# The adaLN products of a mixer kernel in four column groups of the TensorE array

## The chip, the cores and the metric

The kernel runs on one core of a Trainium2 chip. The metric is device time in microseconds (us) of one execution; the kernel before took 1698.51 us, the median of three runs (1695.80 to 1698.83).

## The reference

One layer of an encoder works on 1280 tokens of 1024 channels (a prompt of 1024 rows and a sample of 256, each with its own condition vector c). What the change touches is the first step: a vector of shift and scale for each of the two conditions, which modulates the normalised input ahead of the large projection.

```python
def mixer_layer(x, c, w_ada, b_ada, norm_g, w_in, ...):
    mod = c @ w_ada + b_ada                       # c: (1, 1024), w_ada: (1024, 3072)
    shift, scale, gate = jnp.split(mod[:, None, :], 3, axis=-1)
    h = rms_norm(x, norm_g) * (1.0 + scale) + shift
    p = h @ w_in                                  # (tokens, 1024) @ (1024, 11280)
...
    merged = g_conv * (y_conv @ w_proj_conv) + g_mlstm * (y_m @ w_proj_mlstm)
    return x + gate * (merged @ w_out)
```

All of it is float32. A gated short convolution and a bidirectional mLSTM follow from p; they and the output stage are untouched.

## The kernel before

**The large projection.** h is kept transposed: 1024 channels as eight tiles `xt` of 128 channels, by 1280 tokens in two halves of 640 (columns of the program `b11`, `b12` for the channels 0 to 511, `b21`, `b22` for 512 to 1023). The projection runs as a Strassen scheme on pairs of 128 output columns: seven jobs a pair, each a product of four channel tiles (k = 0 to 3) with 640 tokens. Every operand is split into a rounded part H and a remainder L, so one k of one job is six matmuls of 128x320 (line 770), written `L770 ... wh/wl` below. I call these six **a group**. The moving operands of the jobs are `b00H/L` (that is b11), `b10H/L` (b21), `t2H/L`, `t3H/L`, further `xt` tiles (t1 and t4) and `b11H/L` (b22). The first eight jobs, the "corners", use only b11 and then b21, with weights that were loaded ahead (`raw`, two loads of 256 KB each).

**The beginning.** `beginning()` loads w_ada's shift and scale columns in eight parts, here w0 to w7 (`load_wa(i)`, two loads of 512 KB each: two k tiles, 512 shift and 512 scale columns). w0 to w3 give the first 512 channels, w4 to w7 the second 512. Between them it loads the ten tiles of x. They land in tiles that later hold other things, so the trace shows w5 as `b10H`, w6 as `b10L`, w4 and w7 both as `b11H`; x appears as `t3H`, `t3L`, `b11L`, `t2H`, `t2L`.

**adaLN.** `adaln(i)` multiplies c with part i: for each of two k tiles and each half j (shift, scale) one fp32 matmul with a 128x4 stationary operand `cz4` (two condition columns, two of zeros) and 512 moving columns, accumulated over w0..w3 or w4..w7 into a PSUM tile `acc` of 4 rows in two banks (line 487). After the last part the two 4x512 rows go to SBUF, one by VectorE, one by ScalarE (line 496), are turned into columns by four TensorE transposes each (line 500) and `modulation` makes `s1` and `shf` from them (lines 474 to 476).

**The turns.** `turn_x` transposes one channel tile of two or three token tiles (line 449, 128x128 each) into a PSUM tile `misc`, of which there are two, and ScalarE or VectorE writes it to `xt` with scale and shift (lines 454, 457). `both_parts` splits an `xt` tile into H (ScalarE, 381) and L (VectorE, 382), `combine` forms sums of tiles (VectorE, 387). VectorE also makes sums of weights (`comb`, 642) and adds finished jobs (686).

**What sets the order.** All operations are put on a `Board` with an estimated duration; `order()` plays them by ready times and steps and fixes the order of every engine's queue, and of SyncE's queue (SP), which issues all the loads and stores. The estimates decide the order only; on the chip each engine takes its queue strictly as written and waits for semaphores. The names with numbers in the order rows are buffers.

Of the kernel before, what the change touches and what calls it, by code (L numbers as in the profile page):

```python
# [9 lines left out]
F32 = mybir.dt.float32  # L10
F32R = mybir.dt.float32r
AF = mybir.ActivationFunctionType
ALU = mybir.AluOpType
# [3 lines left out]
P = 128  # L17
D = 1024
KT = D // P
# [21 lines left out]
class Board:  # L41
# [25 lines left out]
    def buf(self, pool, shape, dt, tag, bufs, t=None):  # L67
        b = self.Buf(pool, shape, dt, tag, bufs, t)
        self.places.setdefault((id(pool), tag), []).append(b)
        return b  # L70

    def op(self, eng, us, f, r=(), w=(), after=(), low=False, slack=0.0):

        o = self.Op()
        o.eng, o.us, o.f, o.low, o.step, o.n, o.played, o.slack = eng, us, f, low, self.step, len(self.ops), False, slack
        o.before = set(after)
        for t in r:
            if t in self.writer:
                o.before.add(self.writer[t])
        for t in w:  # L80
            o.before.update(self.readers.get(t, ()))
            if t in self.writer:
                o.before.add(self.writer[t])
        for t in w:
            self.writer[t], self.readers[t] = o, []
        for t in r:
            if t not in w:
                self.readers.setdefault(t, []).append(o)
        o.before.discard(o)
        o.bufs = list(dict.fromkeys(b for t in (*r, *w) for b in (t if isinstance(t, tuple) else (t,)) if isinstance(b, self.Buf)))  # L90
        for b in o.bufs:
            b.users.append(o)
        self.ops.append(o)
        return o
# [87 lines left out]
def encoder_kernel(  # L182
# [7 lines left out]
    V, A, G, PE = nc.vector, nc.scalar, nc.gpsimd, nc.tensor  # L190
# [14 lines left out]
    const = ctx.enter_context(tc.tile_pool(name="const", bufs=1))  # L205
# [20 lines left out]
    ident = const.tile([P, P], F32, name="ident")  # L226
# [67 lines left out]
    s1 = const.tile([P, KT, 2], F32, name="s1")  # L294
    shf = const.tile([P, KT, 2], F32, name="shf")
    board = Board()
    op, buf = board.op, board.buf
# [5 lines left out]
    cp = xstack.enter_context(tc.tile_pool(name="cp", bufs=5))  # L303
# [86 lines left out]
    def beginning():  # L390
        junks = [((lambda b=b: b[:, 0:D]), b) for b in (big(), big())]

        def cz4():
            return junks[0][1][:, D:D + 32].rearrange("p (k s) -> p k s", s=4)

        def load_wa(i):

# [65 lines left out]
        cv_ = cols[:, 0:16].rearrange("p (s k) -> p k s", s=2)  # L463
        ctok = ("c",)
        op("POOL", .15, lambda: G.memset(cz4(), 0.0), w=[junks[0][1], ctok])
        op("DVE", .15, lambda: V.tensor_copy(cz4()[:, :, 0:2], cv_), r=[ctok], w=[ctok])
        pada = {}

        def modulation(hf, pm):

            ks = slice(4 * hf, 4 * hf + 4)
            pmc = pm[:, 0:32].rearrange("p (h k l s) -> p h k l s", h=2, l=2, s=2)[:, :, :, 0]
            wide = (lambda c: cols[:, c + 4 * hf:c + 4 * hf + 4].unsqueeze(2).to_broadcast([P, 4, 2]))
            V.tensor_tensor(out=s1[:, ks], in0=pmc[:, 1], in1=wide(RSH + 8), op=ALU.add)
            V.scalar_tensor_tensor(out=s1[:, ks], in0=s1[:, ks], scalar=1.0, in1=wide(RNG), op0=ALU.add, op1=ALU.mult)
            V.tensor_tensor(out=shf[:, ks], in0=pmc[:, 0], in1=wide(RSH), op=ALU.add)

        def adaln(i):

            hf = i // 4  # L480
            if i == 0:
                pada.update((n, buf(psX, [P, 2, 512], F32, "acc", 3)) for n in range(2))
            t = pada[hf]
            for n, (wa, tok) in enumerate(wa_at[i]):
                kt = 2 * (i % 4) + n
                for j in range(2):
                    op("PE", .88, lambda j=j, kt=kt, wa=wa: PE.matmul(
                        t[0:4, j, :], cz4()[:, kt, :], wa()[:, j * 512:(j + 1) * 512],
                        start=kt == 0, stop=kt == KT - 1), r=[ctok, tok], w=[(t, j)])
            if i % 4 < 3:  # L490
                return
            pm = misc_buf()
            for j in range(2):
                m, f = buf(cp, [P, 4, P], F32, "comb", 5), (V.tensor_copy, A.copy)[j]
                row = (lambda m=m: m[0:4].rearrange("p a b -> p (a b)"))
                op(("DVE", "ACT")[j], .6, lambda j=j, f=f, row=row: f(row(), t[0:4, j, :]), r=[(t, j)], w=[m])

                def turn_mod(j=j, row=row):
                    for r in range(4):
                        PE.transpose(pm[:, 16 * j + 4 * r:16 * j + 4 * r + 4], row()[:, r * P:(r + 1) * P], ident[0:4, 0:4])  # L500

                op("PE", .25, turn_mod, r=[m], w=[(pm, j)])
            op("DVE", .6, lambda: modulation(hf, pm), r=[(pm, 0), (pm, 1)], w=[("s1", hf)])

        def fetch(*items):

            for it in items:
                board.step = -20
                if it[0] == "x":
                    for c in GROUPS[it[1]]:  # L510
                        load_x(c)
                    board.step = -14 if it[1] < 2 else -11
                    norm_x(GROUPS[it[1]])
                elif it[0] == "w":
                    load_wa(it[1])
                    board.step = -18 + it[1] // 4 * 16
                    adaln(it[1])
                else:
                    early_load(*it)
# [55 lines left out]
    def big():  # L575

        return buf(rp, [P, T], F32, "big", 2)

    def misc_buf():
        return buf(psA, [P, 512], F32, "misc", 2)  # L580
# [651 lines left out]
    for st in head_pairs(range(1, NH)):  # L1232
        add(st)

    beginning()
    advance(ends[0] - 10)
    board.step = at[0]
# [26 lines left out]
    for k in range(at[0], len(todo)):  # L1264
        n, m = divmod(k - at[0], 7)
# [365 lines left out]
    def second(s):  # L1631
        h, i = divmod(s - 10, 10)
        return (h, two_[h].order[i], i) if 0 <= h < NH else (None, None, None)
# [3 lines left out]
    for s in range(10 * NH + 15):  # L1637
# [4 lines left out]
        h, c, i = second(s - 3)  # L1642
        if h is not None and h + 2 < NH and c in (5, 7, 9):
            load_head(h + 2, (5, 7, 9).index(c))
        h, i = divmod(s, 10)
# [11 lines left out]
        h, c, i = second(s)  # L1657
        if h is not None:
            g = c - c % 2
# [7 lines left out]
        h, c, i = second(s - 2)  # L1667
        if h is not None:
            prs[h, c - c % 2].values(c)
        h, c, i = second(s - 4)  # L1670
# [185 lines left out]
```

## Time and profile before

| | |
|---|---|
| runs | 1698.51 us median, 1695.80 lowest, 1698.83 highest |
| span of the profiled execution, first to last instruction | 1694.4 us |
| own time of the profiled execution | not given apart; the runs lie 1.4 to 4.4 us above the span |
| TensorE (PE) busy | 1654.8 us, 98% of the span |
| VectorE (DVE), ScalarE (ACT), GpSimd (POOL) busy | 59%, 34%, 40% |
| products of line 770 on the chain that ended last | 61% of the span |
| DMA in the first of 40 slices, and mean | 318 GB/s, 143 GB/s |
| mean granted TensorE clock | 0.996 of full speed |

The profile's page gives for each engine its busy time, for 40 slices of the span its busy tenths, and the chain of work that ended last, followed back step by step to what released it. Its other views, asked for stretches of the trace, list instructions in order of time with their duration and, in brackets, the idle time of the engine before them and what ended it (`[0.88 <-DVE xt L382]`: 0.88 us idle until VectorE's line 382 had written `xt`). An `x8` at the end means that eight such records are merged in the row. A full fp32 matmul leaves two records, a transposition or an fp32r matmul one. Busy times of PE overlap, since its ends are modelled: its starts are the sounder numbers.

### The profile page before, as it was taken

What the parts mean: (1) busy time and instruction counts of PE and PEld (TensorE: products, weight loads), DVE (VectorE), ACT (ScalarE), POOL (GpSimd) and SP (SyncE); (2) the same over time, 40 slices, a digit from 0 to 9 for tenths busy, and PEclk for the clock granted to TensorE, in tenths of its full rate; (3) what the DMA queues carried; (4) which work ended last, traced back from release to release, by engine and by line L of the source; (5) the groups of instructions that cost most, each with busy time, mean ns of one, the idle gap of its engine ahead of it and who ended that gap; (6) DMA issues with size and microseconds to landing.
All of it is one profiled execution on the core that took longest, in us unless ns stands there. A gap on an engine that the chain in (4) does not pass through costs nothing.

```text
span 1694.4 us, 27722 instructions
## 1 busy us (share of the span) xinstructions
PE 1654.8 (98%) x10542; PEld 1567.3 (92%) x10542; DVE 1000.7 (59%) x1696; ACT 577.4 (34%) x1117; POOL 678.6 (40%) x499
## 2 busy tenths in 40 slices
PE   7999999999999999999999999999999999999997
PEld 2799999999999999999999999999988899998985
DVE  4794434456555565566656886652267777565645
ACT  3552332124453222222222211212256565333322
POOL 1133333335664566677666633333210101223412
PEclk9999999999999999999999999999999999999999
DMA  9334325324553122221222556468779855783631
GB/s 318 108 127 137 120 89 124 73 77 124 149 154 103 57 69 69 82 81 61 62 66 82 145 129 141 118 134 289 254 234 293 261 186 158 231 279 119 239 108 63
DMA packets 282681, 241.88 MB, mean 143 GB/s; under 512 B 96196, under 2 KB 237748, under 8 KB 282548
## 3 DMA queue, kind: packets, MB, share of 16 engines
q1 hardware_dynamic: 282368, 240.06, 46.6%
q8 instruction: 84, 1.38, 0.3%
q14 instruction: 49, 0.40, 0.1%
q10 hardware_dynamic: 180, 0.04, 0.0%
HBM read 171.16 MB, written 68.89 MB: 142 GB/s over the span
## 4 chain that ended last, share of the span: by engine, by line
PE 90%; DVE 4%; DMA 3%; SPq 1%; issue 1%; ACT 1%; ACTq 0%; DVEq 0%
PE acc L770 61%; PE qc L1357 3%; PE u L1375 3%; PE accd L1530 2%; PE accd L1531 2%; PE accd L1532 2%; PE accd L1743 2%; PE accd L1744 2%; PE accd L1742 2%; PE acc L1598 2%; PE acc L1597 2%; PE acc L1599 2%; DMA raw<-in_w_in_dram 1%; PE misc L1418 1%; SPq L318 1%; PE misc L1458 1%
## 5 line engine op out<-in xcount | busy, mean ns | idle before, releaser
L330 POOL TENSOR_TENSOR wl<-comb,wh 128x512 fp32r<-128x512 f32 x176 | 247.3, 1405 | 288.0 <-ACT wh L329 279.8
L686 DVE TENSOR_TENSOR q<-acc,q 128x640 f32<-128x640 f32 x272 | 220.8, 819 | 221.5 <-PE acc L770 219.3
L330 POOL TENSOR_TENSOR wl<-raw,wh 128x512 fp32r<-128x512 f32 x136 | 191.8, 1411 | 237.0 <-ACT wh L329 225.2
L770 PE MATMUL acc<-xt,wh 128*128 128x320 f32 x1408 | 265.1, 310 | 2.2 <-DVE xt L382 2.2
L770 PEld LDWEIGHTS acc<-xt,wh 128*128 128x128 f32 x1408 | 220.9, 188 | 3.5 <-DVE xt L382 3.2
L329 ACT CAST wh<-comb 128x512 fp32r<-128x512 f32 x176 | 109.0, 619 | 298.5 <-PE acc L770 282.6
L329 ACT CAST wh<-raw 128x512 fp32r<-128x512 f32 x136 | 84.4, 621 | 271.0 <-PE acc L770 205.5
L770 PE MATMUL acc<-xt,wl 128*128 128x320 f32 x704 | 160.3, 309 | 0.0
L1558 POOL TENSOR_TENSOR wl<-raw,wh 128x512 fp32r<-128x512 f32 x28 | 36.2, 1297 | 233.4 <-ACT wh L1557 227.0
L770 PEld LDWEIGHTS acc<-xt,wl 128*128 128x128 f32 x704 | 117.7, 188 | 0.0
L642 DVE TENSOR_TENSOR comb<-raw 128x512 f32<-128x512 f32 x88 | 73.4, 834 | 41.1 <-DMA raw<-in_w_in_dram 19.1
L837 POOL TENSOR_TENSOR big<-big,q 128x640 f32<-128x640 f32 x48 | 78.3, 1631 | 35.8 <-DVE q L686 27.4
L586 ACT ACTIVATE q<-q,zero 128x640 f32<-128x640 f32 x76 | 63.1, 831 | 78.0 <-DVE q L686 72.3
L642 DVE TENSOR_TENSOR comb<-raw,comb 128x512 f32<-128x512 f32 x44 | 46.0, 1045 | 62.6 <-POOL wl L330 62.6
L770 PE MATMUL acc<-b00H,wh 128*128 128x320 f32 x352 | 81.6, 312 | 0.0
L1530 PE MATMUL accd<-y,wh 128*128 128x320 f32 x256 | 79.9, 313 | 1.5 <-DVE og L1508 1.5
L770 PE MATMUL acc<-b10H,wh 128*128 128x320 f32 x352 | 80.2, 308 | 0.8 <-ACT q L700 0.8
L770 PE MATMUL acc<-b11H,wh 128*128 128x320 f32 x352 | 80.7, 310 | 0.0
L770 PE MATMUL acc<-t2H,wh 128*128 128x320 f32 x352 | 80.4, 310 | 0.0
L770 PE MATMUL acc<-t3H,wh 128*128 128x320 f32 x352 | 80.3, 309 | 0.0
L770 PE MATMUL acc<-t3L,wh 128*128 128x320 f32 x352 | 80.2, 309 | 0.0
L770 PE MATMUL acc<-t3H,wl 128*128 128x320 f32 x352 | 80.2, 309 | 0.0
(307 smaller groups left out, 4144.0 us busy)
## 6 DMA issues: line engine op xcount, KB each, us to landing
raw<-in_w_in_dram SPq DMA_DIRECT2D x108, 256.0 KB
raw<-in_w_in_dram SPq DMA_DIRECT2D x40, 512.0 KB
th<-th_dr SPq DMA_DIRECT2D x32, 320.0 KB
th_dr<-q SPq DMA_DIRECT2D x28, 320.0 KB
raw<-in_w_proj_conv_dram SPq DMA_DIRECT2D x16, 512.0 KB
k<-kn_dr SPq DMA_DIRECT2D x64, 128.0 KB
raw<-in_w_proj_mlstm_dram SPq DMA_DIRECT2D x16, 512.0 KB
raw<-in_w_out_dram SPq DMA_DIRECT2D x16, 512.0 KB
```

The lines of the kernel that those rows point to most:

```text
L329: op("ACT", .63, lambda: A.copy(wh[:], src()), r=r, w=[wh])
L330: op("POOL", 1.4, lambda: G.tensor_tensor(out=wl[:], in0=src(), in1=fp(wh[:]), op=ALU.subtract), r=[*r, wh], w=[wl])
L586: A.activation(out, in_, AF.Tanh, bias=zero[:, 0:1], scale=0.5)
L642: op("DVE", .9, lambda: V.tensor_tensor(out=t[:], in0=x(), in1=y(), op=o), r=[x.tok, y.tok], w=[t])
L686: op("DVE", .82, lambda: V.tensor_tensor(out=two(dst()), in0=acc[:, :, 0:TQ], in1=two(t()), op=ALU.add), r=[acc, t.tok], w=[dst.tok])
L770: PE.matmul(acc[:, q, 0:TQ], st_[:, k_, :], m_[:, q * TQ:(q + 1) * TQ], start=k_ == 0 and n == 0, stop=k_ == 3 and n == 2)
L837: op("POOL", 1.65, lambda: G.tensor_tensor(out=dst(), in0=dst(), in1=t(), op=ALU.mult), r=[dst.tok, t.tok], w=[dst.tok])
L1357: PE.matmul(pq[:, 0:HD + 2], qTs[i][:, kd, c * P:(c + 1) * P], C[:, kd, :], start=kd == 0, stop=kd == 1)
L1375: PE.matmul(pu[:, db, 0:HD + 2], k[:, db * P:(db + 1) * P], wv[:], start=True, stop=True)
L1530: PE.matmul(accs[q][:, :TQ], wh, yH, start=kt == 0, stop=False)
L1531: PE.matmul(accs[q][:, :TQ], wh, yL, start=False, stop=False)
L1558: op("POOL", 1.36, lambda wh=wh, wl=wl, src=src: G.tensor_tensor(out=wl[:], in0=src(), in1=fp(wh[:]), op=ALU.subtract), r=[raw, wh], w=[wl])
```

## The change

The stationary operand becomes 32 columns wide (two condition columns, 30 of zeros; `cz4` grows from 128x32 to 128x256). The four matmuls of a part (two k tiles by two halves j) go to four groups of 32 columns of the array, `tile_position=(0, g)` with g = 32 (2n + j), and so to four groups of 32 partitions of one PSUM bank. Each group accumulates its own k tiles over the four parts, so the sum over n is left open. At the end one VectorE copy takes the whole 128x512 bank to SBUF, and four small matmuls with the constant `sel` (128x4: ones that pick and add the partitions of both n for each j and condition) turn it into columns and add the two parts in one step. ScalarE's copy is gone, `modulation` reads another layout, and the Board's estimates change from .88 us for one matmul to 1.1 us for two.

```diff
-            return junks[0][1][:, D:D + 32].rearrange("p (k s) -> p k s", s=4)
+            return junks[0][1][:, D:D + 256].rearrange("p (k s) -> p k s", s=32)
...
+        sel = const.tile([P, 2, 2], F32, name="sel")
+        half = (lambda i: ident[:, 64 * i:64 * i + 64].rearrange("p (j r) -> p j r", r=32)[:, :, 0:2])
+        op("DVE", .15, lambda: V.tensor_tensor(out=sel[:], in0=half(0), in1=half(1), op=ALU.add), w=["sel"])
...
-                for j in range(2):
-                    op("PE", .88, lambda j=j, kt=kt, wa=wa: PE.matmul(
-                        t[0:4, j, :], cz4()[:, kt, :], wa()[:, j * 512:(j + 1) * 512],
-                        start=kt == 0, stop=kt == KT - 1), r=[ctok, tok], w=[(t, j)])
+                def mm(n=n, kt=kt, wa=wa):
+                    for j in range(2):
+                        g = 32 * (2 * n + j)
+                        PE.matmul(t[g:g + 32, 0, :], cz4()[:, kt, :], wa()[:, j * 512:(j + 1) * 512],
+                                  start=i % 4 == 0, stop=i % 4 == 3, tile_position=(0, g))
+
+                op("PE", 1.1, mm, r=[ctok, tok], w=[t])
...
-                op(("DVE", "ACT")[j], .6, lambda j=j, f=f, row=row: f(row(), t[0:4, j, :]), r=[(t, j)], w=[m])
...
-                        PE.transpose(pm[:, 16 * j + 4 * r:16 * j + 4 * r + 4], row()[:, r * P:(r + 1) * P], ident[0:4, 0:4])
...
+            op("DVE", .65, lambda: V.tensor_copy(m[:].rearrange("p a b -> p (a b)"), t[:, 0, :]), r=[t], w=[m])
...
+                    PE.matmul(pm[:, 4 * r:4 * r + 4], m[:, r, :], sel[:].rearrange("p j s -> p (j s)"), start=True, stop=True)
```

Since the estimates and the dependencies change, the order of the queues changes with them, in the first 125 us or so; behind that every engine's row is the same as before.

On SP, the loads around w7 (`b11H<-in_w_ada`, two of 512 KB; the `raw` rows are weights of the corners, 256 KB each). Before:

```order
L318 DMA b10H<-in_w_ada_dram 128x2x512 x2
L318 DMA b10L<-in_w_ada_dram 128x2x512 x2
L318 DMA raw<-in_w_in_dram 128x4x128 x2
L318 DMA b11H<-in_w_ada_dram 128x2x512
L318 DMA raw<-in_w_in_dram 128x4x128 x2
L318 DMA b11H<-in_w_ada_dram 128x2x512
```

And with the change:

```order
L318 DMA b10H<-in_w_ada_dram 128x2x512 x2
L318 DMA b10L<-in_w_ada_dram 128x2x512 x2
L318 DMA raw<-in_w_in_dram 128x4x128 x2
L318 DMA b11H<-in_w_ada_dram 128x2x512 x2
L318 DMA raw<-in_w_in_dram 128x4x128 x2
```

The second half of w7 is issued ahead of two weight loads that it stood behind.

On PE, from the end of w6 to the first turns of the later tokens (`t2H`, `t2L`). Before:

```order
L487 MATMUL acc<-b10H,big 4x512 x4
L487 MATMUL acc<-b10L,big 4x512 x4
L487 MATMUL acc<-b11H,big 4x512 x4
L500 MATMUL misc<-ident,comb 128x4 x4
L449 MATMUL misc<-ident,t2H 128x128 x2
L449 MATMUL misc<-ident,t2L 128x128
L500 MATMUL misc<-ident,comb 128x4 x4
```

And with the change:

```order
L774 MATMUL acc<-b00H,wh 128x320 x2
L774 MATMUL acc<-b00L,wh 128x320 x2
L774 MATMUL acc<-b00H,wl 128x320 x2
L493 MATMUL acc<-b11H,big 32x512 x4
L774 MATMUL acc<-b00H,wh 128x320 x2
L774 MATMUL acc<-b00L,wh 128x320 x2
L774 MATMUL acc<-b00H,wl 128x320 x2
L504 MATMUL misc<-sel,comb 128x4 x4
L449 MATMUL misc<-ident,t2H 128x128 x2
L449 MATMUL misc<-ident,t2L 128x128
```

Seven groups of the corners now stand ahead of the small products (L504), where four stood ahead of the first L500; further down, among the turns, one group more stands ahead of the last turn than before, and four fewer behind it.

On DVE, around the first two sums of weights for the second full Strassen pair (`comb<-raw`, then `comb<-comb,raw`). Before:

```order
L387 TENSOR_TENSOR xt<-xt 128x640 x2
L686 TENSOR_TENSOR q<-acc,big 128x640
L642 TENSOR_TENSOR comb<-raw 128x512
L642 TENSOR_TENSOR comb<-comb,raw 128x512
L382 TENSOR_TENSOR t3L<-xt,t3H 128x640
L686 TENSOR_TENSOR q<-acc,big 128x640
```

And with the change:

```order
L382 TENSOR_TENSOR t2L<-xt,t2H 128x640 x2
L690 TENSOR_TENSOR q<-acc,big 128x640
L646 TENSOR_TENSOR comb<-raw 128x512
L646 TENSOR_TENSOR comb<-comb,raw 128x512
L387 TENSOR_TENSOR xt<-xt 128x640
L690 TENSOR_TENSOR q<-acc,big 128x640
L387 TENSOR_TENSOR xt<-xt 128x640 x3
L382 TENSOR_TENSOR t3L<-xt,t3H 128x640 x4
```

Four operations L387 that stood ahead of the two sums now stand behind them: counted from the last turn's L457, VectorE takes 20 rows ahead of the first sum instead of 24, and 13 instead of 17 ahead of the sum that is the last to read the tile which the next pair's load waits for. One sum of weights that stood ahead of the last token splits (of t4) now stands behind them.

More of the change, by code (lines that the diff above doesn't have):

```diff
@@ L467, in beginning @@
         pada = {}
+        sel = const.tile([P, 2, 2], F32, name="sel")
+        half = (lambda i: ident[:, 64 * i:64 * i + 64].rearrange("p (j r) -> p j r", r=32)[:, :, 0:2])
+        op("DVE", .15, lambda: V.tensor_tensor(out=sel[:], in0=half(0), in1=half(1), op=ALU.add), w=["sel"])
         def modulation(hf, pm):
             ks = slice(4 * hf, 4 * hf + 4)
-            pmc = pm[:, 0:32].rearrange("p (h k l s) -> p h k l s", h=2, l=2, s=2)[:, :, :, 0]
+            pmc = pm[:, 0:16].rearrange("p (k h s) -> p h k s", h=2, s=2)
             wide = (lambda c: cols[:, c + 4 * hf:c + 4 * hf + 4].unsqueeze(2).to_broadcast([P, 4, 2]))
@@ L485, in adaln, with turn_mod @@
                 kt = 2 * (i % 4) + n
-                for j in range(2):
-                    op("PE", .88, lambda j=j, kt=kt, wa=wa: PE.matmul(
-                        t[0:4, j, :], cz4()[:, kt, :], wa()[:, j * 512:(j + 1) * 512],
-                        start=kt == 0, stop=kt == KT - 1), r=[ctok, tok], w=[(t, j)])
+                def mm(n=n, kt=kt, wa=wa):
[4 more added lines that the diff above has]
+                op("PE", 1.1, mm, r=[ctok, tok], w=[t])
             if i % 4 < 3:
                 return
[L492 to L503, printed above, removed]
+            pm, m = misc_buf(), buf(cp, [P, 4, P], F32, "comb", 5)
+            op("DVE", .65, lambda: V.tensor_copy(m[:].rearrange("p a b -> p (a b)"), t[:, 0, :]), r=[t], w=[m])
+            def turn_mod():
+                for r in range(4):
+                    PE.matmul(pm[:, 4 * r:4 * r + 4], m[:, r, :], sel[:].rearrange("p j s -> p (j s)"), start=True, stop=True)
+            op("PE", .9, turn_mod, r=[m, "sel"], w=[pm])
+            op("DVE", .6, lambda: modulation(hf, pm), r=[pm], w=[("s1", hf)])
         def fetch(*items):
```

## The prediction

> **What bounds the kernel now.** I read the page's busy times first, then the granted clock and busy times by stretch, then the chain that ended last, then the engines in order of time where the chain leaves PE.
>
> ```profile
> PE 1654.8 (98%) x10542; PEld 1567.3 (92%) x10542; DVE 1000.7 (59%) x1696; ACT 577.4 (34%) x1117; POOL 678.6 (40%) x499
> ...
> core 0: us, PE busy (x) PEld busy (x) DVE busy (x) ACT busy (x) POOL busy (x), PEclk, DMA share, GB/s
> 28.00:30.27 2.27, 0.77 (x8) 0.44 (x7) 0.70 (x2) 1.56 (x3) 2.27 (x2) 1.00 1.05 379
> 30.27:33.68 3.41, 3.41 (x6) 0.40 (x6) 1.16 (x4) 1.04 (x2) 2.52 (x3) 0.50 1.04 409
> 50.00:51.00 1.00, 1.00 (x4) 0.09 (x1) 0.00 (x0) 0.00 (x0) 0.00 (x0) 1.00 0.62 219
> 51.00:52.00 1.00, 0.29 (x1) 0.00 (x0) 0.00 (x0) 0.00 (x0) 0.00 (x0) 1.00 0.08 31
> 110.00:120.00 10.00, 7.78 (x47) 6.90 (x48) 9.69 (x11) 3.43 (x7) 2.86 (x2) 1.00 0.18 53
> 200.00:300.00 100.00, 100.00 (x684) 99.81 (x683) 38.91 (x52) 29.02 (x43) 35.03 (x28) 1.00 0.39 105
> ```
>
> Over the whole span PE is the bound. The change lies in the first 55 us, and there the bounds are others: DMA runs full until about 51 us (219, then 31 GB/s in the last stretches), and from 110 to 120 us VectorE is busy 9.69 of 10 us while PE idles 2.2. Only behind that does PE run without a gap.
>
> ```profile
> 45.67 6.71 DMA b11H<-in_w_ada_dram
> 52.43 1.88 PE acc L487 x4
> ...
> 61.10 1.93 DVE xt L387
> 63.03 0.60 DVE xt L457
> ...
> 65.32 0.55 PE misc L449 x5
> 65.86 0.89 PE acc L770 x6
> ...
> 75.46 3.04 DVE b11L L382 x4
> ...
> 92.28 5.34 DMA raw<-in_w_in_dram
> ...
> 115.35 1.94 DVE xt L382
> 117.33 182.17 PE acc L770 x1240
> ```
>
> The chain says what a saving on PE is worth. It runs over DMA to the landing of w7, over PE for the turns (one group .89 us, five transpositions .55), then from 75.46 to 117.33 almost wholly over VectorE, and then over PE for 182 us. **What counts is therefore when VectorE gets through its token splits, not how much PE work is taken out.** A shift at 117 us should reach the end undiminished, since the queues behind are the same.
>
> **The change part by part.** First the landing of w7.
>
> ```profile
> 38.90 1.06 SPq L318 DMA_DIRECT2D b11H<-in_w_ada_dram  x1
> 40.05 5.53 SPq L318 DMA_DIRECT2D raw<-in_w_in_dram  x2
> 45.67 0.86 SPq L318 DMA_DIRECT2D b11H<-in_w_ada_dram  x1
> ```
>
> ```profile
> 41.64 3.60 PE L487 MATMUL acc<-b10H,big 128*4 128x512 f32 x8
> 45.07 3.60 PE L487 MATMUL acc<-b10L,big 128*4 128x512 f32 x8
> 49.41 1.88 PE L487 MATMUL acc<-b11H,big 128*4 128x512 f32 x4 [0.75 <-DMA b11H<-in_w_ada_dram]
> 52.43 1.88 PE L487 MATMUL acc<-b11H,big 128*4 128x512 f32 x4 [1.14 <-DMA b11H<-in_w_ada_dram]
> 54.31 0.38 PE L500 MATMUL misc<-ident,comb 4*128 4x4 f32 x4
> 54.62 0.44 PE L449 MATMUL misc<-ident,t2H 128*128 128x128 f32 x2
> 55.10 0.41 PE L500 MATMUL misc<-ident,comb 4*128 4x4 f32 x4
> 55.44 0.57 PE L770 MATMUL acc<-b00H,wh 128*128 128x320 f32 x2
> 63.67 0.44 PE L449 MATMUL misc<-ident,t3H 128*128 128x128 f32 x2 [1.29 <-DVE xt L457]
> 74.98 0.27 PE L449 MATMUL misc<-ident,t2L 128*128 128x128 f32 x1
> ```
>
> The two halves of w7 land 52.43 - 49.41 = 3.02 us apart, with two weight loads of 256 KB between them, together as many bytes as one half. With the change these come behind, so the second half lands 1.5 us earlier, at 50.9 (bounds: 0 if the lanes share out otherwise, 1.5).
>
> The products. Four take 45.07 - 41.64 = 3.43 us, eight passes of .43; two take 1.71. If two on different column groups don't overlap it stays 1.71; if they overlap wholly it is .86. Each product's own two passes go to the same columns and can't overlap; the next product's first pass may run beside the second pass. That is three steps, 1.28 us, which I take. For w0 to w6 the saving is worth nothing by itself, since the wait for the next load takes it up. It lets three groups (2.65 us) move into this stretch.
>
> A rule bears on this. The Trainium skill, "TensorEngine Tiling (Array Packing)", section "Key Properties", says that tiles work independently and that a change of the tiling mode drains the engine. No run here shows either yet. By the first alone the sum below would be better by .4 us; the second has no price there, and would be part of the upper bound of the small products.
>
> The way to the modulation. One VectorE copy of 128x512 stands for two of 4x512, at the same length per partition.
>
> ```profile
> 5.02 0.24 DVE L254 COPY cols<-misc 128x80 f32<-128x80 f32 x1 [4.13 <-PE misc L253]
> 53.49 0.68 DVE L496 COPY comb<-acc 4x512 f32<-4x512 f32 x1 [5.92 <-PE acc L487]
> 56.85 1.13 DVE L457 TENSOR_SCALAR xt<-misc,s,shf 128x256 f32<-128x256 f32 x2 [0.86 <-PE misc L449]
> 73.97 1.13 DVE L457 TENSOR_SCALAR xt<-misc,s,shf 128x256 f32<-128x256 f32 x2 [1.02 <-PE misc L449]
> 78.41 4.13 DVE L387 TENSOR_TENSOR xt<-xt 128x640 f32<-128x640 f32 x4
> 91.58 0.68 DVE L642 TENSOR_TENSOR comb<-raw 128x512 f32<-128x512 f32 x1
> 97.71 0.69 DVE L642 TENSOR_TENSOR comb<-raw 128x512 f32<-128x512 f32 x1 [1.10 <-DMA raw<-in_w_in_dram]
> 113.83 0.68 DVE L642 TENSOR_TENSOR comb<-raw 128x512 f32<-128x512 f32 x1
> 114.43 4.70 DVE L382 TENSOR_TENSOR xt<-xt 128x640 fp32r<-128x640 f32 x4
> ```
>
> w7's product ends at 50.9 + 1.28 = 52.2. A handoff is about .14 (53.49 + .68 to the L500 at 54.31), the copy .68, so the small products start at 53.15; the group of .89 that stands between is done by then and costs nothing. The four small products are full fp32 with 128 columns of weights, so eight passes. A transposition with as many weights takes .11 (.55 for five): .88 us, the value I take. Bounds: .38, as for the old four, and 1.76, eight times the .22 of one t2H record. They end at 54.0, where the first `t2H` turn now starts, against 54.62: **-.6 us**. The second L500 is gone (55.10 to 55.44): **-.34**.
>
> The turns. Between this point and the last turn (74.98) there is one group more: **+.89**. PE idled 1.29 us at 63.67 for the VectorE row at 63.03, which stood behind the slow combination at 61.10. In the new queue that combination comes after it, so I take the 1.29 as gone (bounds 0 and 1.29): **-1.29**. At the last turn that is -1.34.
>
> VectorE's stretch from there to the last split (114.43 + 4.70) has the same operations but one sum of weights, now behind the splits (the .68 of 113.83): **-.68**. It also has the wait for `raw` at 97.71. VectorE, which came to it at 96.6, now has four operations L387 fewer ahead of it, of 1.03 each (the four at 78.41), and starts 1.34 earlier: 91.2. The load is issued when the last sum that reads its tile is done (the row at 91.58, done at 92.2, then 5.34 to the landing). That sum too has four operations fewer ahead, so I put it 5.1 to 5.4 earlier and the landing at 92.5. The wait would be 1.3 instead of 1.10: **+.2**.
>
> Sum: -.6 - .34 + .89 - 1.29 - .68 + .2 = **-1.8 us**. PE, four groups ahead (3.5 us), only waits longer in front of t1 and t4, where it idled 2.2 us before.
>
> Costed at nothing: the wider clear of `cz4` and the sum for `sel`, since VectorE waits 4.13 us at that time for the rows of c (row 5.02), and ScalarE's copy, which stood beside VectorE's. Uncovered, the longest would cost a copy, .68.
>
> The bounds of this case: with whole overlap, small products at .38 and the raw wait gone, -1.8 - .4 - .5 - 1.3 = -4.0; with no gain in landing, no overlap, small products at 1.76 and the stall kept, -1.8 + 1.5 + .4 + .9 + 1.3 = +2.3.
>
> **The rivals.**
>
> A, PE's lead counts in full. If VectorE uses up its idle time between 57 and 75 us, of which four rows name PE's transpositions (the first at 56.85, the last at 73.97; with the two between them 2.99 us), it gains that on top of the .94 of the start and the .68: -4.6, so 1693.9. For: those waits are for PE. Against: in the turns PE's queue is as dense as before, one group to every five transpositions, and sets the pace. Its limit is PE's whole saving, -1.34 - 3.5 - 2.2 = -7.0.
>
> B, nothing overlaps on PE, or its clock falls. Without overlap, w5 and w6 hold PE from 41.6 to 48.5, two groups to 50.3, w7 to 53.7, and the small products end at 55.5 instead of 54.0: -.3, so 1698.2. The same comes of a fall in the clock: in 28.00 to 30.27 PE was busy .77 of 2.27 us, and the next 3.41 us ran at .50. PE with shorter products and a wait of some 3 us in front of t1 can meet this again; it costs half of 3.41, 1.7 us, leaving -.1. The Trainium skill, "TensorE: Matmul & The Clock Gate", section "The HAM clock gate (the "warmup" mystery)", gives the window as about 3.4 us, and the row agrees with 3.41.
>
> C, VectorE waits for `raw`. The sums that need this load now stand ahead of all that t3, t1 and t4 need. If the load lands no earlier than before, at 97.6 (because SP stands at a store or a weight load ahead of it), VectorE waits 6.4 us instead of 1.3: -1.8 + 5.1 = +3.3, so 1701.8. It decides from a landing later than 94.3. For: the load's issue waits for VectorE itself and stands behind others in SP's queue. Against: these others follow PE's progress, which is ahead.
>
> **How the numbers follow.** The span is 1694.4, the median 1698.5, the lowest run 1695.8; what lies around the span is 1.4 to 4.1 us, and I set the sum against the median: 1698.5 - 1.8 = **1696.7**. Chances: forecast .56, A .18, B .16, C .10. The range 1693.0 to 1700.5 leaves out about half of A and most of C. A measurement of this kernel tells some .2% (3.4 us) from no change. Faster by more: A and a tail of the forecast, .24. Slower by more: half of C, and what I haven't seen, .09. Within: .67.
>
> **What would show it.** After the change the second half of w7 is read at about 51 us, a pair of products starts its second product before the first would have ended, the small products end near 54, the last turn (`t2L`, `b11L`) lies near 73.6, and VectorE's last four splits before b11H end near 117.3. If PE waits more than before in front of t1 and t4, the bound was VectorE's, as argued. What would make it wrong: a VectorE wait over 3 us at the first `comb<-raw` of the second pair (C), VectorE's last splits before 115 us (A), or rows at half clock behind 50 us (B).

## The result and the profile after

| | before | after |
|---|---|---|
| median of 15 runs each | 1696.67 us (1695.18 to 1698.83) | 1694.41 us (1690.88 to 1696.66) |
| ratio, 95% interval | | 0.9981 [0.9974, 0.9988] |
| span of the profiled execution | 1694.4 us | 1690.4 us |

The ratio makes the change -3.2 us (-4.4 to -2.0); the means of the fifteen runs lie 3.3 us apart (1696.99 and 1693.70), the medians 2.3. The expected part came and more, and a part was given back on PE. Two runs of the later experiments were far longer than the others of their kernel (5799.75 us of the kernel before, 1811.34 of e3) and are left out of the ratios.

First SyncE's queue and PE in order of time after the change (start, duration, line, operation, idle before and what ended it), from the loads of w7 to the last turn. Lines of the kernel stand 4 later than before from `adaln` on (L487 is L493, L500 is L504, L770 is L774).

```profile
37.26 1.79 SPq L318 DMA_DIRECT2D raw<-in_w_in_dram  x2
39.25 3.17 SPq L318 DMA_DIRECT2D b11H<-in_w_ada_dram  x2
42.52 3.41 SPq L318 DMA_DIRECT2D raw<-in_w_in_dram  x2
```

```profile
49.18 1.05 PE L493 MATMUL acc<-b11H,big 128*32 128x512 f32 x4
50.60 1.05 PE L493 MATMUL acc<-b11H,big 128*32 128x512 f32 x4 [0.37 <-DMA b11H<-in_w_ada_dram]
51.59 0.56 PE L774 MATMUL acc<-b00H,wh 128*128 128x320 f32 x2
...
52.57 0.95 PE L504 MATMUL misc<-sel,comb 128*128 128x4 f32 x8
53.38 0.42 PE L449 MATMUL misc<-ident,t2H 128*128 128x128 f32 x2
...
72.37 0.27 PE L449 MATMUL misc<-ident,t2L 128*128 128x128 f32 x1
...
107.26 0.90 PE L774 MATMUL acc<-xt,wh 128*128 128x320 f32 x2 [3.42 <-DVE xt L382]
...
116.54 0.45 PE L774 MATMUL acc<-b11H,wh 128*128 128x320 f32 x2
```

w7's two halves are now issued together, ahead of two weight loads, and the second is read at 50.60 instead of 52.43. Two products (x4) hold PE for 51.59 - 50.60 = .99 us. The last `t2L` turn comes at 72.37 instead of 74.98. But in front of t1 PE waits 3.42 us, and the product behind is slow: two fp32r matmuls in .90 us.

The other side of that wait is VectorE. Its rows after the change, then GpSimd's of the same time after and before (x: merged records):

```profile
91.32 0.69 DVE L646 TENSOR_TENSOR comb<-raw 128x512 f32<-128x512 f32 x1 [0.83 <-DMA raw<-in_w_in_dram]
...
106.39 3.02 DVE L382 TENSOR_TENSOR xt<-xt 128x640 fp32r<-128x640 f32 x4
109.33 0.81 DVE L690 TENSOR_TENSOR q<-acc,big 128x640 f32<-128x640 f32 x1
110.07 3.60 DVE L382 TENSOR_TENSOR xt<-xt 128x640 fp32r<-128x640 f32 x4
```

```profile
104.05 1.74 POOL L330 TENSOR_TENSOR wl<-comb,wh 128x512 fp32r<-128x512 f32 x1 [1.90 <-ACT wh L329]
119.02 2.55 POOL L330 TENSOR_TENSOR wl<-comb,wh 128x512 fp32r<-128x512 f32 x2 [13.23 <-ACT wh L329]
```

```profile
106.66 1.79 POOL L330 TENSOR_TENSOR wl<-comb,wh 128x512 fp32r<-128x512 f32 x1 [0.78 <-ACT wh L329]
110.18 1.58 POOL L330 TENSOR_TENSOR wl<-comb,wh 128x512 fp32r<-128x512 f32 x1 [1.73 <-ACT wh L329]
115.32 1.28 POOL L330 TENSOR_TENSOR wl<-comb,wh 128x512 fp32r<-128x512 f32 x1 [3.55 <-ACT wh L329]
```

Before, the four splits of t1 and the four of t4 took 4.12 and 4.70 us; the second row is one of t1's four by itself:

```profile
109.06 4.12 DVE L382 TENSOR_TENSOR xt<-xt 128x640 fp32r<-128x640 f32 x4
110.53 1.92 DVE L382 TENSOR_TENSOR xt<-xt 128x640 fp32r<-128x640 f32 x1
```

Now they take 3.02 and 3.60, while GpSimd stands idle for 13.23 us; before, it worked three times in that stretch. A single split takes .81 us. Before, one in each four took 1.92 (at 110.53 and 115.35), beside GpSimd's rows of 110.18 and 115.32; after the change none does. So VectorE is through at 110.07 + 3.60 = 113.67 us instead of 114.43 + 4.70 = 119.13: 5.46 us earlier, three times the predicted lead. PE made less of it. Its busy time and granted clock (PEclk) after the change, in stretches of 3.41 us that are cut where the clock changes (105.86 and 112.69):

```profile
core 0: us, PE busy (x) PEld busy (x) DVE busy (x) ACT busy (x) POOL busy (x), PEclk, DMA share, GB/s
...
102.44:105.86 3.42, 1.40 (x10) 1.14 (x8) 3.42 (x5) 2.12 (x4) 1.74 (x1) 1.00 0.33 123
105.86:109.27 3.41, 2.01 (x7) 2.01 (x8) 3.41 (x5) 1.28 (x2) 0.00 (x0) 0.50 0.00 0
109.27:112.69 3.42, 3.42 (x14) 3.42 (x14) 3.21 (x5) 0.16 (x1) 0.00 (x0) 0.50 0.00 0
112.69:116.10 3.41, 3.41 (x26) 3.41 (x24) 2.34 (x4) 0.83 (x1) 0.00 (x0) 1.00 0.00 0
```

At half clock PE ran 14 matmuls in a full stretch, where it runs 26 at full clock. The first product with b11H behind t4, where PE has caught up, is at 116.54 against 119.88 before:

```profile
119.88 0.46 PE L770 MATMUL acc<-b11H,wh 128*128 128x320 f32 x2
```

I call this **the join**. Its shift, -3.34 us, stands in the chain of waits as far as the long run of products that starts at 376.12 (379.46 before); .3 us is lost again in the 582 us of that run, ahead of the wait for `th`:

```profile
1167.82 6.83 DMA th<-th_dr
```

Before, that row starts at 1170.84, 3.02 later. Behind it the same code took 521.9 to 525.1 us in the eleven profiles of this study (e5 and e7 left out), so a span alone tells less than the join does.

### The profile page after: what moved, and what is told of

It reads as the page before. It is cut to its first block, busy times and chain, and to the rows that moved or that the text cites. A ratio compares the mean times of both kernels' runs of the same rounds, so it can differ in the third digit from the quotient of the medians.

```text
span 1690.4 us, 27717 instructions
## 1 busy us (share of the span) xinstructions
PE 1644.9 (97%) x10542; PEld 1568.7 (93%) x10542; DVE 997.1 (59%) x1697; ACT 576.4 (34%) x1115; POOL 677.5 (40%) x499
## 4 chain that ended last, share of the span: by engine, by line
PE 91%; DVE 3%; DMA 3%; ACT 1%; issue 1%; SPq 1%; ACTq 0%; DVEq 0%
PE acc L774 62%; PE qc L1361 3%; PE u L1379 3%; PE accd L1534 2%; PE accd L1535 2%; PE accd L1536 2%; PE accd L1748 2%; PE accd L1746 2%; PE accd L1747 2%; PE acc L1601 2%; PE acc L1602 2%; PE acc L1603 2%; DMA b11H<-in_w_ada_dram 1%; PE misc L1422 1%; PE misc L1462 1%
## 5 line engine op out<-in xcount | busy, mean ns | idle before, releaser
L774 PE MATMUL acc<-xt,wh 128*128 128x320 f32 x1408 | 266.0, 311 | 3.4 <-DVE xt L382 3.4
L774 PEld LDWEIGHTS acc<-xt,wh 128*128 128x128 f32 x1408 | 222.6, 189 | 3.9 <-DVE xt L382 3.7
L774 PE MATMUL acc<-xt,wl 128*128 128x320 f32 x704 | 161.3, 310 | 0.0
L774 PEld LDWEIGHTS acc<-xt,wl 128*128 128x128 f32 x704 | 118.5, 189 | 0.0
L774 PE MATMUL acc<-b00H,wh 128*128 128x320 f32 x352 | 81.9, 314 | 0.0
L774 PE MATMUL acc<-b10H,wh 128*128 128x320 f32 x352 | 80.4, 309 | 0.8 <-ACT q L704 0.8
L774 PE MATMUL acc<-b11H,wh 128*128 128x320 f32 x352 | 81.1, 312 | 0.0
L774 PE MATMUL acc<-b00L,wh 128*128 128x320 f32 x352 | 80.2, 309 | 0.1
L774 PE MATMUL acc<-t3H,wh 128*128 128x320 f32 x352 | 80.3, 309 | 0.0
L774 PE MATMUL acc<-t2L,wh 128*128 128x320 f32 x352 | 80.2, 309 | 0.0
L774 PE MATMUL acc<-t3H,wl 128*128 128x320 f32 x352 | 80.2, 309 | 0.0
```

The costliest lines, as they stand in the source:

```text
L774: PE.matmul(acc[:, q, 0:TQ], st_[:, k_, :], m_[:, q * TQ:(q + 1) * TQ], start=k_ == 0 and n == 0, stop=k_ == 3 and n == 2)
```

## The experiments

My theory after the result: the gain is (1) the order of the loads, which brings w7 earlier, (2) the shorter stretch up to the last turn, (3) VectorE's splits, which GpSimd no longer slows, less (4) about 2 us at half clock. Rivals are named with each. "The fourth kernel" is e4. Lines that an experiment adds shift the numbers in its rows. The join is that of one execution, the ratio that of all runs; the third column says how far the profiled run lies from the median of its kernel's runs.

| kernel | join, us | profiled run against its median, us | ratio to before, 95% interval |
|---|---|---|---|
| before | 119.88 | | 1 |
| after | 116.54 | -2.3 | 0.9981 [0.9974, 0.9988] |
| e1: before, PE's order near after's | 121.92 | +2.8 | 0.9999 [0.9990, 1.0008] |
| e3: after, w7's second half behind the weights | 118.90 | -2.9 | 1.0001 [0.9993, 1.0010] |
| e8: before, weights behind w7 | 119.98 | +1.9 | 0.9990 [0.9981, 0.9999] |
| e2: after, order of PE near before's | 122.30 | +1.2 | 1.0010 [1.0001, 1.0018] |
| e4: after, clock kept | 114.48 | -0.1 | 0.9972 [0.9962, 0.9982] |
| e10: e8, clock kept | 118.56 | -0.3 | 0.9995 [0.9986, 1.0003] |
| e11: e3, clock kept at t1 | 117.91 | -0.8 | 0.9983 [0.9974, 0.9992] |
| e6: e4, GpSimd busy | 118.35 | +1.8 | 0.9987 [0.9979, 0.9996] |
| e9: e4, w7 further ahead | 112.97 | -2.6 | 0.9962 [0.9949, 0.9974] |

**e1: only the order, with the products of before.** The Board's estimate of one product is lowered, so that PE's queue comes out close to that of after; the second half of w7 stays behind the two weight loads.

```diff
-                    op("PE", .88, lambda j=j, kt=kt, wa=wa: PE.matmul(
+                    op("PE", .55, lambda j=j, kt=kt, wa=wa: PE.matmul(
```

> The kernel before, with the single 128x4 products, but with the Board's estimate for one product at .55 instead of .88, which by itself brings seven groups of the corners ahead of the last small transpositions, as the change does; the two halves of w7 keep the two weight loads between them. Theory 1 (order and landing): w7's second half still lands at 52.4, the products still take 1.7, the last turn lies near 75.2 as before; but VectorE's queue is nearly that of the change, so its splits of t4 end 1 to 2.5 us earlier than 119.1, and the time falls by 1 to 2 us (ratio to before .9988 to .9994). Theory 2 (the column groups themselves bring the gain): no gain, ratio 1.000.

Measured: 0.9999 [0.9990, 1.0008]. As timed, the order by itself brings nothing that can be told from zero. The trace shows two parts that cancel, in the last turn and in VectorE's splits:

```profile
77.67 0.27 PE L449 MATMUL misc<-ident,t2L 128*128 128x128 f32 x1
```

```profile
111.77 3.02 DVE L382 TENSOR_TENSOR xt<-xt 128x640 fp32r<-128x640 f32 x4
...
115.44 3.59 DVE L382 TENSOR_TENSOR xt<-xt 128x640 fp32r<-128x640 f32 x4
```

From the last turn to its last split VectorE takes 115.44 + 3.59 - 77.67 = 41.36 us, where it took 44.15 before and takes 41.30 after the change. So the order alone, with single products, gives VectorE its whole gain of 2.8 us in this stretch, the short splits included. But the last turn comes 2.69 us later than before: PE is late with the single products and reads w7's second half only at 55.91, without a wait for its load. Some 1.7 us of that are half clock while it multiplies w5 (42.97 to 46.39) in this execution, the slowest of its eleven. The wait in front of t1 grew to 3.48 us and the clock fell behind it, as after the change.

**e2: the grouped products, with an order of PE near before's.**

```diff
-                op("PE", 1.1, mm, r=[ctok, tok], w=[t])
+                op("PE", 1.76, mm, r=[ctok, tok], w=[t])
```

> The change with its Board estimate for two products at 1.76 instead of 1.1, so that the order comes near that of before: four groups ahead of the small products, and two weight loads between the halves of w7; the products still run in four column groups. Theory 1: w7's second half lands at 52.4, the products take 1.0, the first t2H turn starts at 55.0 instead of 53.4, and the time falls by 0 to 1 us (ratio .9994 to 1.000). Theory 2: most of the 3.2 us stay (ratio near .998).

Measured: 1.0010 [1.0001, 1.0018]. PE in order of time, and its clock by stretches:

```profile
49.86 1.92 PE L493 MATMUL acc<-b11H,big 128*32 128x512 f32 x4 [2.71 <-DMA b11H<-in_w_ada_dram]
52.87 1.92 PE L493 MATMUL acc<-b11H,big 128*32 128x512 f32 x4 [1.09 <-DMA b11H<-in_w_ada_dram]
```

```profile
45.40:48.80 3.40, 1.36 (x6) 0.14 (x4) 1.09 (x2) 0.72 (x1) 0.00 (x0) 1.00 1.12 328
48.80:52.20 3.40, 1.92 (x4) 0.19 (x4) 0.00 (x0) 0.00 (x0) 0.00 (x0) 0.50 0.58 188
...
59.00:62.40 3.40, 3.40 (x15) 3.36 (x15) 1.31 (x3) 0.64 (x1) 0.00 (x0) 0.50 0.00 0
```

With shorter products and the old order PE stands idle for most of 45.40 to 48.80 (busy 1.36 of 3.40), and from there to 62.40 it runs at half clock. The first `t2H` turn then starts at 58.05 instead of the 55.0 expected. Here faster products were worth less than nothing, since PE then waited for loads.

**e3: only the order of the loads undone.** In the kernel after, SyncE issues w7's second half behind the two weight loads, as before.

```diff
...
+            i = seq.index(self.w7b)
+            j = [n for n in range(i + 1, len(seq)) if seq[n].eng == "SP"][1]
+            seq.insert(j, seq.pop(i))
...
```

> The change with one thing undone: SP issues the second half of w7 behind the two weight loads, as before; every other queue is the same. Theory 1: the landing moves from 50.6 to about 52.4 and all behind it by 1.5 to 1.8 us as far as the products of b22 (116.5 to 118.2), ratio to before .9990 to .9992. Rival: PE and VectorE have slack behind the landing that takes it up, ratio stays .998.

Measured: 1.0001 [0.9993, 1.0010]; as timed, the gain is gone.

```profile
52.72 1.05 PE L500 MATMUL acc<-b11H,big 128*32 128x512 f32 x4 [0.52 <-DMA b11H<-in_w_ada_dram]
...
55.50 0.42 PE L456 MATMUL misc<-ident,t2H 128*128 128x128 f32 x2
```

The read is 2.12 us later than after the change, so is the first turn (53.38 there), and the join is 2.36 later. In front of t1 PE waits 3.74 us here, and its clock falls there too (108.14 to 114.96).

**e8: only the order of the loads done, in the kernel before.** My first two attempts (e5 in the kernel before, ratio 1.008, and e7 in e4, 1.0039) moved w7's load itself forward in the program, past products that read w4 from the same tile: these then read w7's data instead of w4's, and PE waited 15.48 us in the middle of w4 (e5). Their times say nothing on the order of the loads. e8 moves the two weight loads back instead.

```diff
...
+            ws = [o for o in seq[:seq.index(self.w7b)] if o.eng == "SP"][-2:]
+            for o in ws:
+                seq.remove(o)
+            i = seq.index(self.w7b) + 1
+            seq[i:i] = ws
...
```

> The kernel before, with SyncE's two weight loads of 256 KB, which stood between the two halves of w7, put behind the second half, and nothing else. Theory 1 (most of the gain of the change is this order): PE reads the second half at about 50.8 us instead of 52.43, the last turn t2L follows 1.5 us earlier at about 73.5 instead of 74.98, the first product with b11H behind t4 (119.88 before) comes at 118.0 to 118.5, and the ratio is 0.9988 to 0.9993, unless PE's wait before t1 grows past 3.4 us, when half clock gives back up to 2 us. Rival (the order is worth something only with PE's shorter products): the second half lands earlier, but the last turn stays within 0.5 us of 74.98 and the ratio is 1.000.

Measured: 0.9990 [0.9981, 0.9999].

```profile
49.32 3.60 PE L496 MATMUL acc<-b11H,big 128*4 128x512 f32 x8
52.92 0.38 PE L509 MATMUL misc<-ident,comb 4*128 4x4 f32 x4
53.24 0.44 PE L458 MATMUL misc<-ident,t2H 128*128 128x128 f32 x2
...
73.56 0.27 PE L458 MATMUL misc<-ident,t2L 128*128 128x128 f32 x1
```

PE reads both halves without a wait, and the first turn starts at 53.24, no later than after the change. The last turn is at 73.56, 1.42 earlier than before, and the last splits end 1.33 earlier (113.09 + 4.71). In this profiled execution all of it was lost again to half clock at the end of t4, without a wait of PE over .90 us. The stretch of half clock and the one of the same length ahead of it:

```profile
113.14:116.56 3.42, 1.74 (x11) 1.45 (x11) 3.21 (x4) 0.62 (x1) 1.29 (x1) 1.00 0.53 156
116.56:119.97 3.41, 3.41 (x14) 3.41 (x14) 2.60 (x4) 1.06 (x2) 0.00 (x0) 0.50 0.00 0
```

And the kernel before at the same place, cut in the same way, in steps of 3.413 us from the clock change at 30.27 in its own trace:

```profile
112.19:115.60 3.41, 2.32 (x14) 2.06 (x15) 3.31 (x6) 1.35 (x2) 0.28 (x1) 1.00 0.00 0
115.60:119.01 3.41, 2.53 (x17) 2.23 (x16) 3.20 (x3) 0.00 (x0) 1.00 (x1) 1.00 0.54 156
```

PE's waits are about as long there, but they fall otherwise on the steps: in e8 .78 and .90 us lie in one step and leave 1.74 us busy, before .78 and .88 lie in two steps, which leaves 2.32 and 2.53, and the clock stays. The profiled execution is the slowest of e8's eleven; its mean clock is .995, and eight of the others have .997 or .998. So the ratio shows more of the lead than this join does.

**e4: the clock kept.** The kernel after, with 18 matmuls of 128x320 between t3 and t1 whose result is never read.

```diff
...
+                for _ in range(18):
+                    PE.matmul(idle[:, 0:TQ], m[:, 0:P], m[:, 0:TQ], start=True, stop=True)
...
```

> The change with 18 matmuls of 128x320 put on PE between t3 and t1, into a PSUM tile that nobody reads, where PE waits 3.4 us for VectorE and then runs at half clock. Theory 1: they take 2.65 us of that wait, the clock stays full, t1 and t4 take .88 a group as far as VectorE's splits allow, the first product of b22 comes at about 114.4 instead of 116.5: 2.1 us less than the change, ratio to before .9969. Rival: VectorE's splits set the pace there anyway (they end at 113.7), so at most .5 us less, ratio .998.

Measured: 0.9972 [0.9962, 0.9982].

```profile
103.80:107.20 3.40, 2.70 (x19) 2.43 (x17) 3.40 (x4) 1.54 (x3) 1.80 (x1) 1.00 0.16 61
107.20:110.60 3.40, 3.26 (x22) 3.27 (x23) 3.40 (x6) 1.46 (x2) 0.00 (x0) 1.00 0.00 0
```

```profile
107.34 0.57 PE L774 MATMUL acc<-xt,wh 128*128 128x320 f32 x2 [0.84 <-DVE xt L382]
...
114.48 0.46 PE L774 MATMUL acc<-b11H,wh 128*128 128x320 f32 x2
```

t1 starts as late as after the change (107.34 against 107.26), since it waits for VectorE, but at full clock, and the join is 2.06 us earlier. More work on PE makes the kernel faster. The two ratios' intervals overlap, so it is the trace that shows this, and the ratio that doesn't speak against it.

**e10 and e11: e8 and e3 with the clock kept**, to see whether the parts add up. e10 puts three times four unread matmuls into the waits of t1 and t4, e11 the 18 of e4 into e3.

```diff
...
+                if n == 0 and (k, k_) in ((14, 2), (15, 0), (15, 1)):
+                    for _ in range(4):
+                        PE.matmul(idle[0][:, 0:TQ], st_[:, k_, :], m_[:, 0:TQ], start=True, stop=True)
...
```

> The kernel with the products of before and the two weight loads behind w7 (the e8 kernel), with three times four matmuls of 128x320, whose result is never read, put where PE waits for VectorE's splits in t1 and t4. Theory (the landing alone is worth 1.3 to 1.5 us at b11H, and e8 lost it to half clock): no row at half clock from 113 to 121 us, the first product with b11H behind t4 at 118.3 to 118.6 instead of 119.98, and the ratio 0.9980 to 0.9987 instead of 0.999. Rival (the dummies don't keep the clock, or the landing's lead is lost elsewhere): the product stays at 119.5 or later, ratio 0.999 to 1.000.

> The kernel after with w7's second half behind two weight loads again (the e3 kernel), with the 18 unread matmuls between t3 and t1 that keep PE at work (as in the fourth kernel). Theory (three parts that add up: landing, grouped products with their order, clock): no half clock at t1, the first product with b11H behind t4 at 116.6 to 116.9 instead of 118.90, so 2.1 to 2.4 us behind the fourth kernel's 114.48, and the ratio 0.9980 to 0.9988, that is 1.2 to 2.0 us better than e3's 1.0001. Rival (e3 timed worse than its profile for another reason than the clock at t1, for instance half clock in the first 60 us): the product comes earlier in the profile, but the ratio stays at 0.9995 or more.

Measured: e10 0.9995 [0.9986, 1.0003], e11 0.9983 [0.9974, 0.9992]. In e10's trace the clock stays full and the join is at 118.56, 1.32 earlier than before, as expected; the ratio is at least 1.4 us worse than expected and no better than e8's, most of whose runs, by their mean clocks, had little half clock to win back. The loads' order alone is therefore worth 1.3 us at the join; timed it is 1.7 (e8) and .8 (e10), with intervals that end close to nothing or reach it. In e11 the ratio is as expected and the join 1.0 us later than expected. PE lost that ahead of the turns, where this execution fell to half clock at w7's second half:

```profile
52.41 1.50 PE L500 MATMUL acc<-b11H,big 128*32 128x512 f32 x4 [1.97 <-DMA b11H<-in_w_ada_dram]
```

So the parts don't simply add up: with the clock kept, the loads' order brings 1.3 us at the join of the old kernel, the grouped products with their order of PE and VectorE 2.0 (e11), and both together 5.4 (e4). About 1.1 of the difference is e11's half clock at w7: its last turn is at 75.58, e3's at 74.47. The other 1.0 fits with the loads' order being worth more to the changed kernel (2.36 at the join, e3): there PE waits for w7's second half and reads it 2.12 us sooner, while in e8 PE is itself busy until about 51.0, 1.4 sooner than before. As timed, the unread matmuls are worth 3 us to e3 (1.0001 to .9983, intervals apart), so half clock took what its second part brought.

**e6: GpSimd busy beside the splits.** e4, with six additions of 128x320 on GpSimd, never read.

```diff
...
+                for _ in range(6):
+                    op("POOL", .05, lambda: G.tensor_tensor(out=gcol[:].rearrange("p a b h c -> p (a b h c)")[:, 0:320], in0=B21[3][:, 0:320], in1=B21[3][:, 0:320], op=ALU.add),
...
```

> The fourth kernel (PE kept at work before t1) with six GpSimd additions of 128x320, whose result is never read, placed beside VectorE's splits for t1 and t4 (about 106 to 112 us), where GpSimd idles after the change and worked before it. Theory (VectorE's rows there are shorter after the change because GpSimd is idle): the four splits of t1 go from 3.02 us to about 3.6 to 4.1 and the four of t4 from 3.60 to about 4.1 to 4.7, the first product with b11H behind t4 goes from 114.5 to 115.5 to 116.7, and the ratio from 0.9972 to 0.9979 to 0.9985. Rival (the rows are shorter for another reason): 3.02 and 3.60 stay, the product comes at 114.5 and the ratio is 0.997.

Measured: 0.9987 [0.9979, 0.9996]. GpSimd's rows, then VectorE's:

```profile
108.26 7.74 POOL L570 TENSOR_TENSOR gcol<-xt 128x320 f32<-128x320 f32 x6 [1.50 <-DVE xt L387]
```

```profile
108.10 4.59 DVE L382 TENSOR_TENSOR xt<-xt 128x640 fp32r<-128x640 f32 x4
112.62 0.81 DVE L693 TENSOR_TENSOR q<-acc,big 128x640 f32<-128x640 f32 x1
113.35 4.26 DVE L382 TENSOR_TENSOR xt<-xt 128x640 fp32r<-128x640 f32 x4
```

The same splits take 4.59 and 4.26 us instead of 3.02 and 3.60, 2.23 more, so work on GpSimd lengthens them. VectorE's additions out of PSUM keep their .81. The join is 3.87 later; the other 1.6 us were lost ahead of t1, where the additions don't run, and are not theirs. (1.1 of them is a second split of t3 that took 1.92 us, beside one of GpSimd's weight splits.)

**e9: further along the same way.** e4, with two more weight loads moved behind w7 (the ones at 37.26 in the rows of SyncE above).

```diff
...
+            ws = [o for o in seq[:seq.index(self.w7[0])] if o.eng == "SP"][-2:]
...
+            i = seq.index(self.w7[1]) + 1
+            seq[i:i] = ws
...
```

> The fourth kernel (PE kept at work before t1) with two more weight loads of 256 KB, which stood in front of both halves of w7 in SyncE's queue, put behind them. Theory 1 (what counts is when w7's second half lands): PE reads it at about 49.3 to 49.8 us instead of 50.6, the last turn t2L comes 0.8 to 1.3 us earlier than after the change (72.37), the first product with b11H behind t4 at about 113.2 to 113.7 instead of 114.5, and the ratio is 0.9964 to 0.9968. Rival (VectorE between the last turn and t1, or a weight load that now comes late, takes it back): the product stays at 114.5 or comes later, and the ratio is 0.997 or more.

Measured: 0.9962 [0.9949, 0.9974], the best kernel of the study in five runs, faster than before and, by the median, than after (1690.69 us).

```profile
49.11 1.06 PE L502 MATMUL acc<-b11H,big 128*32 128x512 f32 x8
50.11 0.56 PE L783 MATMUL acc<-b00H,wh 128*128 128x320 f32 x2
...
51.90 0.42 PE L458 MATMUL misc<-ident,t2H 128*128 128x128 f32 x2
...
112.97 0.46 PE L783 MATMUL acc<-b11H,wh 128*128 128x320 f32 x2
```

Both halves of w7 wait for PE now, the first turn is 1.48 us earlier than after the change, and the join 1.51 earlier than e4's: between the turns and the join nothing takes a lead back.

## Why the prediction was right, and where its steps were not

The predicted change was -1.8 us, the measured one -3.2 (-4.4 to -2.0): the direction is right, the size too small. The time, 1694.41 against 1696.7, lies inside the range. Most of that gap isn't the change at all: I started from 1698.51, the median of three runs, and the kernel before has 1696.67 over fifteen, so on that base the forecast would be 1694.9. That the total came out near is luck in part: it rests on two omissions of about 2 us each and of opposite sign, VectorE's shorter splits and PE's half clock. Two of the three signs that I had named for being wrong came, last splits before 115 us and half clock behind 50 us.

- **The landing of w7** (50.9 predicted, 50.60 measured): right. Undone, it costs the changed kernel 2.4 us at the join and all its gain as timed (e3); alone, it gives the old kernel 1.3 us at the join (e10).
- **Two products in column groups** (1.28 us taken, .99 measured): I let one product of two overlap only in part; they run side by side. Two take .99 us, two passes of .43 and .13 that I can't place. The Trainium skill, "TensorEngine Tiling (Array Packing)", section "Key Properties", has the tiles independent of each other; the rows agree, down to four products (x8) in 50.11 - 49.11 = 1.00 us in e9 against 3.43 for four in one group. The loss that a change of mode brings by the same section can't be told from these rows.
- **The small products** (.88): .81 (52.57 to 53.38). The first turn comes 1.24 earlier instead of .6, from the terms above.
- **One group more, the second L500 gone, the stall of 1.29 gone**: right in mechanism; the row at 63.67 with its 1.29 has no counterpart after the change. The last turn moved by 2.61 instead of 1.34: .64 from the earlier start, .63 in short gaps of PE's queue that I didn't break down.
- **VectorE's stretch** (-.68 + .2): the sum of weights went behind the splits, and the wait for `raw` is .83 instead of the 1.3 predicted. What failed is "the same operations": I gave the eight splits their old durations. They shrank by 1.10 + 1.10 us, one lengthened row in each four, because the changed order also moved GpSimd's weight splits away from them: with single products the same order gives 3.02 and 3.59 (e1), and work put there on GpSimd brings long rows back (e6).
- **"A shift at 117 us should reach the end"**: from the join on it does. What failed is the step in front of it, that PE "only waits longer in front of t1 and t4". The wait reached 3.42 us and the clock fell to .50: the second half of rival B, which I had priced at 1.7 and given .16. It costs 2.06 (e4). I had treated it as a case apart from a VectorE lead, though the lead is what makes the wait longer.

The sum at the join, with its measured terms: last turn -2.61, sum of weights -.68, splits -2.20, wait for `raw` 0.83 - 1.10 = -.27, other rows of VectorE +.30, together -5.46 at VectorE's last split. PE's join lay .75 behind that before and 2.87 after: +2.12. That leaves -3.34.

**Rival A** was half there: VectorE's last splits ended before 115 us, though not because it used up its waits for PE: in the turns these are .60, 1.64 and 1.02 us after the change, 3.26 in all against 2.99. **Rival C** didn't come: the load landed at about 91.3, ahead of the 92.5 I reckoned with, and far from 97.6. (The chances count C once as mostly and once as half outside the range; its stated time, 1701.8, lies outside.)

Open: no run joins the new order and the moved loads with the single products, so what the column groups themselves are worth isn't isolated; e1 shows only that this order with single products makes the last turn late. Why the same kernel runs at half clock in some executions and not in others is open in part: the last section says how far the traces explain it. The .3 us lost between the join and `th`, and a disagreement of some 1 us between join and ratio for single kernels (e3, e11) stay open.

## What to carry to other kernels

Look first at what a change does to the order of the loads and of the other engines' queues: here neither the new order (e1) nor the faster products in the old order (e2) gained alone, and of the 5.4 us that both bring together with the moved loads and the clock kept, 2.2 are subtractions on VectorE from which GpSimd's work moved away. When PE gets ahead of the engine that feeds it, read the granted clock behind its waits: here a wait of 3.42 us cost 2.06 us more, which unread matmuls in it brought back, and in e8 two waits of .78 and .90 us, close together, were enough. One profiled execution can be the slowest of its kernel, as with e1 and e8: compare it with the other runs before reading a join as the gain. On VectorE, an operation's duration from the trace holds only as long as GpSimd works beside it as it did.

## What the runs showed of the hardware that was not expected

- Four fp32 products of 128x512 with 32-column weights, in four column groups, take 1.00 us together, the time of little more than one; in one group they take 3.43.
- The clock falls without a full idle window: in e2 PE was busy 1.36 of 3.40 us (45.40 to 48.80), in e8 1.74 of 3.42. The Trainium skill, "TensorE: Matmul & The Clock Gate", section "The HAM clock gate (the "warmup" mystery)", has a window of about 3.4 us; the traces agree, with steps of 3.413.
- In each trace the stretches at half clock start on one grid with steps of 3.413 us and last one or more of them. The grid runs on through the trace (before, one stretch starts at 30.27 and the next at 1457.04, 418 steps later) and lies differently in each execution. Cut on that grid, from 26 to 130 us in all thirteen traces, 17 of the 18 steps at full clock in which PE was busy for at most .57 of the step were followed by half clock (the exception is e7, .50 at 116.23), and none of those at .60 or more. So what a gap costs depends on where the grid cuts it. This isn't the whole rule: ahead of 26 us and behind 1150 us, steps with less than .57 also kept the clock (e8: .45 at 1174.69).
- A VectorE subtraction of 128x640 between SBUF tiles takes .81 us with GpSimd idle. Beside GpSimd's work single ones take 1.92 (110.53 before) or 1.34 (e6, 110.09), others still .81. An addition that reads PSUM took .81 in both cases.
